# Chunk states of an SSD scan in three rounded products, split at the end of each chunk's front

## The chip, the core and the metric

The kernel runs on one core of one Trainium2 chip. Five engines work side by side, each through its own list of instructions: TensorE (PE, with its weight loads as PEld), VectorE (DVE), ScalarE (ACT), GpSimd (POOL) and SyncE (SP), which here only issues transfers. The metric is the device time of one execution in microseconds. Before the change it is 2855.78 us, the median of three runs between 2853.89 and 2859.62.

## The reference

The program is a two-layer decoder over 1024 tokens with 16 learned tokens in front (1040 in all), 1024 features, in float32. Layer 0 is a state-space mixer (SSD) with a gated convolutional feed-forward block, layer 1 a stick-breaking attention with another such block. The change touches only the scan inside the mixer:

```python
cb = jnp.einsum('bclgn,bcsgn->bgcls', c_c, b_c)
y_diag = jnp.einsum('bgcls,bgecls,bcsgep->bclgep', cb, decay_in, xdt)
decay_to_end = jnp.exp(a_cs[..., -1:] - a_cs)
chunk_states = jnp.einsum('bclgn,bgecl,bclgep->cbgepn', b_c, decay_to_end, xdt)
...
_, prev_states = lax.scan(step, ..., (chunk_states, chunk_decay))
y_off = jnp.einsum('bclgn,cbgepn,bgecl->bclgep', c_c, prev_states, jnp.exp(a_cs))
```

There are four groups of eight heads; a head has 64 channels and a state of 128 by 64. `chunk_states` is what a chunk of tokens adds to the state, `y_diag` what a chunk's tokens give each other, `y_off` what the state from earlier chunks gives them.

## The kernel before

The 1040 tokens are cut in two ways. Projections go over three token tiles of 348, 348 and 344; the scan goes over nine chunks, eight of 116 tokens and one of 112. `mixer` runs the scan of one group at a time, chunk by chunk, and fills each chunk with projection tiles of other groups: `SHARES` gives the number of tiles per chunk (mostly 2 in groups 0 and 3, a pattern of 4, 3, 3 in groups 1 and 2). One tile is 24 matmuls, three for each of eight blocks of features: `mm3` multiplies the rounded high part of the weights by the high and the low part of the data, and the low part of the weights by the high part of the data, all of type float32r. Its tiles are called `pj`; they take turns in three PSUM banks.

What comes out of a `pj` tile is convolved by one ACT instruction (L336) and three DVE instructions (L339) and passed through silu (L614), or, for the gate, goes through silu (L646) and is multiplied and squared (L653, L658, L662, L664). Weights of the next block are loaded ahead; ACT rounds them into `wh` (L196), POOL subtracts to get `wl`.

In this stretch the order on PE, DVE, ACT and POOL is the order in which the program is written: a manual schedule switches the framework's own ordering off. The order of one chunk c is:

- the front (`ssd_front`): PE makes `cb` and transposes b and x (`px`); ACT copies the transposed b into `bk` (L778); DVE makes `cbm`, `xdt` and the masked decays `D` (L780, L782, L783); POOL makes `xde`, which is `xdt` times the decay to the chunk's end, in two pieces of 256 columns (the helper's line, L102);
- the projection tiles of this chunk, with the decays of chunk c+1 between them: `D` is loaded, DVE subtracts and clips (L752, eight instructions), ACT takes the exponential (L753);
- the back (`ssd_back`): PE multiplies `S` = bk by xde (L799), then the products `y` (L810, L812); DVE adds `S` to the running state (L805; in chunk 0 ACT copies it, L803), then adds `y` into x (L814); POOL scales the state for the next chunk (`state`, two pieces).

POOL's product `E` for chunk c+1 (the factor of `y_off`, four pieces) stands, in groups 0 and 3, behind the scaled state of chunk c and in front of `xde` of chunk c+1. In most chunks of groups 1 and 2, which have three or four tiles, it has been made before.

Of the kernel before, what the change touches and what calls it, by code (L numbers as in the profile page):

```python
# [8 lines left out]
F32 = mybir.dt.float32  # L9
F32R = mybir.dt.float32r  # L10
AF = mybir.ActivationFunctionType
ALU = mybir.AluOpType

P = 128
# [7 lines left out]
CH = [(c * CB, min(CB, L - c * CB)) for c in range(9)]  # L22
# [32 lines left out]
GH = 8  # L55
# [36 lines left out]
def pieces(eng, out, x, y, op):  # L92

    n = out.shape[1]
    size = 1
    for d in out.shape[2:]:
        size *= d
    step = max(1, PIECE // size)
    done = []
    for a in range(0, n, step):  # L100
        c = slice(a, min(a + step, n))
        done.append(eng.tensor_tensor(out[:, c], x[:, c], y[:, c], op=op))  # L102
    return done


class Trunk:
# [652 lines left out]
    def ssd_front(self, g, x, bt, ct, c, dk, pool):  # L759

        nc = self.nc
        h0 = GH * g
        tt = nc.vector.tensor_tensor
        t0, n = CH[c]
        cc = 3 * (c % 3) + c // 3
        e = t0 + n
        pcb = self.sm("cb")
        if c < 8:
            nc.tensor.transpose(pcb[:n, P : 2 * P], bt[:, t0:e], self.ident)
        nc.tensor.matmul(pcb[:n, :n], bt[:, t0:e], ct[:, t0:e], start=True, stop=True)  # L770
        px = self.lg("px")
        for q in range(4):
            nc.tensor.transpose(px[:n, q * P : q * P + P], x[q][:, t0:e], self.ident)
        px = px[:n].rearrange("p (h d) -> p h d", h=GH)
        bk = xde = None
        if c < 8:
            bk = pool.tile([P, P], F32, tag="bk", name=self.nm("bk"), bufs=2)
            nc.scalar.activation(bk[:n], pcb[:n, P : 2 * P], AF.Copy)  # L778
        cbm = pool.tile([P, CB], F32, tag="cbm", name=self.nm("cbm"), bufs=2)
        tt(cbm[:n, :n], pcb[:n, :n], self.past[:n, :n], op=ALU.mult)  # L780
        xdt = pool.tile([P, GH, 64], F32, tag="xdt", name=self.nm("xdt"), bufs=2)
        tt(xdt[:n], px, self.cols[:n, 0, cc, h0 : h0 + GH].unsqueeze(2).to_broadcast([n, GH, 64]), op=ALU.mult)  # L782
        tt(dk, dk, cbm[:n, :n].unsqueeze(1).to_broadcast([n, GH, n]), op=ALU.mult)  # L783
        if c < 8:
            xde = pool.tile([P, GH, 64], F32, tag="xde", name=self.nm("xde"), bufs=2)
            pieces(nc.gpsimd, xde[:n], xdt[:n], self.cols[:n, 2, cc, h0 : h0 + GH].unsqueeze(2).to_broadcast([n, GH, 64]), ALU.mult)
        return xdt, xde, bk

    def ssd_back(self, g, x, c, dk, ce, xdt, xde, bk, states, pool):

        nc = self.nc
        h0 = GH * g
        t0, n = CH[c]
        cc = 3 * (c % 3) + c // 3
        e = t0 + n
        state, new = states
        if c < 8:
            ps = self.lg("S")
            nc.tensor.matmul(ps, bk[:n], xde[:n].rearrange("p h d -> p (h d)"), start=True, stop=True)  # L799
            psv = ps.rearrange("p (h d) -> p h d", h=GH)  # L800
            if c == 0:
                new = pool.tile([P, GH, 64], F32, tag="state", name=self.nm("state"), bufs=2)
                nc.scalar.activation(new, psv, AF.Copy)  # L803
            else:
                nc.vector.tensor_tensor(new, new, psv, op=ALU.add)  # L805
        py = self.sm("y")
        for i in range(GH):
            q, r = i // 2, 64 * (i % 2)
            y = py[r : r + 64, q * CB : q * CB + n]
            nc.tensor.matmul(y, xdt[:n, i, :], dk[:, i, :], start=True, stop=c == 0)  # L810
            if c:
                nc.tensor.matmul(y, state[:, i, :], ce[:, i, :], start=False, stop=True)  # L812
        for q in range(4):
            nc.vector.scalar_tensor_tensor(x[q][:, t0:e], x[q][:, t0:e], self.par("d_skip", 4 * g + q),  # L814
                                           py[:, q * CB : q * CB + n], op0=ALU.mult, op1=ALU.add)
        scaled = None
        if c < 7:
            scaled = pool.tile([P, GH, 64], F32, tag="state", name=self.nm("state"), bufs=2)
            cn = 3 * ((c + 1) % 3) + (c + 1) // 3
            pieces(nc.gpsimd, scaled, new, self.cd[:, cn, h0 : h0 + GH].unsqueeze(2).to_broadcast([P, GH, 64]), ALU.mult)  # L820
        return new, scaled
# [1236 lines left out]
```

## Time and profile before

| | |
|---|---|
| median of three runs | 2855.78 us |
| the profiled execution's own time | 2855.13 us |
| its span in the trace | 2853.3 us |
| PE busy | 2809.2 us, 98% of the span |
| DVE, ACT, POOL busy | 2065.4, 1580.2, 1578.6 us |
| share of PE in the chain that ended last | 91% |
| granted TensorE clock | 0.997 |
| scan of the four groups | from 114 to 613 us of the span |

The page gives busy time by engine and the chain of work that ended last; the timeline gives each engine's instructions in order with the idle time in front of each, and the name of what ended it. Columns of a timeline row are: start in us from the span's start, length in us, engine, line, operation, output and inputs, shapes, count, and in brackets the idle time before it. `S` is listed as two matmul records for each instruction (64 records for 32 chunks), because the hardware takes a float32 product in two records here.

### The profile page before, as it was taken

Reading aid. Unit: us, or ns where it says so; the run is one execution under the profiler, and the core shown is the slowest. Engines: PE = TensorE matmul, PEld = TensorE weight load, DVE = VectorE, ACT = ScalarE, POOL = GpSimd, SP = SyncE. Lnnn points to the kernel's source line nnn. Section 1 sums busy time; section 2 is a strip of 40 time slices with the busy share of each in tenths; the row PEclk is TensorE's granted clock in tenths of the full one; section 3 lists DMA queues with packets and bytes.
Section 4 is the critical chain, followed back from the end, with each engine's and each line's share of the span. In section 5 each row is a group of like instructions: output and inputs, shape, how many; then the busy total and the mean of one; then the engine's idle time right before and its main releaser. Section 6 shows DMA issues by size and latency. Waiting matters only on the chain.

```text
span 2853.3 us, 56464 instructions
## 1 busy us (share of the span) xinstructions
PE 2809.2 (98%) x21251; PEld 2691.9 (94%) x21251; DVE 2065.4 (72%) x3936; ACT 1580.2 (55%) x3077; POOL 1578.6 (55%) x2144
## 2 busy tenths in 40 slices
PE   8999999999999999999999999999999999999998
PEld 7989999999999999999999999999899999999888
DVE  5676666668487676767886888888749676766776
ACT  5554554543256555555335777777536555555433
POOL 2366455553519888867763212112254888886881
PEclk9999999999999999999999999999999999999999
DMA  4333333343413222235142222222532222225331
GB/s 119 86 112 93 121 83 125 116 136 101 120 64 96 78 80 78 79 135 176 49 142 77 74 73 69 80 70 57 184 131 77 82 80 82 75 82 185 111 104 67
DMA packets 141740, 281.78 MB, mean 99 GB/s; under 512 B 16307, under 2 KB 71740, under 8 KB 141468
## 3 DMA queue, kind: packets, MB, share of 16 engines
q1 hardware_dynamic: 135844, 267.01, 29.8%
q0 software_dynamic: 2048, 6.49, 0.6%
q10 hardware_dynamic: 3576, 4.67, 0.5%
q8 instruction: 168, 2.75, 0.4%
q14 instruction: 104, 0.85, 0.1%
HBM read 207.79 MB, written 55.42 MB: 92 GB/s over the span
## 4 chain that ended last, share of the span: by engine, by line
PE 91%; DVE 4%; ACT 2%; POOL 1%; issue 1%; DMA 0%; SPq 0%; ACTq 0%; DVEq 0%; POOLq 0%
PE p L209 10%; PE p L210 10%; PE p L211 10%; PE acc L209 8%; PE acc L211 8%; PE acc L210 8%; PE pj L209 8%; PE pj L210 8%; PE pj L211 8%; PE po L1710 3%; PE lg L1653 2%; PE wT L1687 2%; PE y L810 1%; PE S L799 1%; PE y L812 1%; PE ms L1069 1%
## 5 line engine op out<-in xcount | busy, mean ns | idle before, releaser
L102 POOL TENSOR_TENSOR wl<-w,wh 128x256 fp32r<-128x256 f32 x760 | 678.9, 923 | 352.2 <-ACT wh L196 225.4
L209 PE MATMUL pj<-uh,wh 128*128 128x348 f32 (+2 forms) x1536 | 500.4, 326 | 2.1 <-DVE xbc L339 1.4
L210 PE MATMUL pj<-ul,wh 128*128 128x348 f32 (+2 forms) x1536 | 494.9, 322 | 0.8 <-DVE ul L320 0.8
L211 PE MATMUL pj<-uh,wl 128*128 128x348 f32 (+2 forms) x1536 | 492.0, 320 | 0.0
L209 PE MATMUL p<-bh,fh 128*128 128x262 f32 (+1 forms) x1408 | 400.9, 285 | 3.9 <-DVE p L1237 3.7
L211 PE MATMUL p<-bh,fl 128*128 128x262 f32 (+1 forms) x1408 | 401.0, 285 | 0.9 <-POOL fl L102 0.9
L210 PE MATMUL p<-bl,fh 128*128 128x262 f32 (+1 forms) x1408 | 399.2, 284 | 0.0
L102 POOL TENSOR_TENSOR fl<-x,fh 128x256 fp32r<-128x256 f32 x352 | 264.3, 783 | 186.8 <-ACT fh L1174 160.9
L210 PE MATMUL p<-bl,wh 128*128 128x262 f32 (+1 forms) x1040 | 295.6, 284 | 1.1 <-DVE bl L1098 1.1
L209 PE MATMUL p<-bh,wh 128*128 128x262 f32 (+1 forms) x1040 | 295.3, 284 | 0.4 <-ACT ft L1234 0.4
L211 PE MATMUL p<-bh,wl 128*128 128x262 f32 (+1 forms) x1040 | 294.1, 283 | 0.0
L209 PEld LDWEIGHTS pj<-uh,wh 128*128 128x128 f32 x1536 | 288.7, 188 | 4.5 <-ACT xbc L336 1.7
L210 PEld LDWEIGHTS pj<-ul,wh 128*128 128x128 f32 x1536 | 289.2, 188 | 2.4 <-DVE ul L320 1.4
L211 PEld LDWEIGHTS pj<-uh,wl 128*128 128x128 f32 x1536 | 288.7, 188 | 0.1
L339 DVE SCALAR_TENSOR_TENSOR c<-p,params,c 128x260 f32<-128x260 f32 (+1 forms) x528 | 248.4, 480 | 54.7 <-ACT c L336 48.3
L209 PEld LDWEIGHTS p<-bh,fh 128*128 128x128 f32 x1408 | 268.0, 191 | 4.7 <-DVE p L1237 4.1
L211 PEld LDWEIGHTS p<-bh,fl 128*128 128x128 f32 x1408 | 267.1, 190 | 1.6 <-POOL fl L102 1.5
L210 PEld LDWEIGHTS p<-bl,fh 128*128 128x128 f32 x1408 | 267.8, 190 | 0.5 <-DVE bl L1098 0.4
L1234 ACT ACTIVATE ft<-p 128x262 f32<-128x262 f32 (+1 forms) x352 | 133.2, 382 | 179.9 <-DVE p L1237 110.1
L210 PE MATMUL acc<-gl,wh 128*128 128x260 f32 (+1 forms) x672 | 214.2, 320 | 0.0
L211 PE MATMUL acc<-gh,wl 128*128 128x260 f32 (+1 forms) x672 | 213.2, 319 | 0.0
L209 PE MATMUL acc<-gh,wh 128*128 128x260 f32 (+1 forms) x672 | 210.8, 320 | 0.1
(336 smaller groups left out, 7690.6 us busy)
## 6 DMA issues: line engine op xcount, KB each, us to landing
w<-in_w_up SPq DMA_DIRECT2D x88, 512.0 KB
w<-in_w_down SPq DMA_DIRECT2D x44, 512.0 KB
w<-in_w_in SPq DMA_DIRECT2D x40, 512.0 KB
E<-ea_d SPq DMA_DIRECT2D x32, 464.0 KB
D<-acs_d SPq DMA_DIRECT2D x32, 420.5 KB
g<-c SPq DMA_DIRECT2D x88, 130.0 KB
g<-c SPq DMA_DIRECT2D x88, 128.0 KB
b<-g SPq DMA_DIRECT2D x16, 520.0 KB
```

Of the source, the lines that this page charges most:

```text
L102: done.append(eng.tensor_tensor(out[:, c], x[:, c], y[:, c], op=op))
L209: self.behind(mm(out, wh, uh, start=first, stop=False, skip_group_check=joins), tie, "behind the sums of squares")
L210: mm(out, wh, ul, start=False, stop=False, skip_group_check=joins)
L211: self.last_mm = mm(out, wl, uh, start=False, stop=last, skip_group_check=joins)
L339: ins = nc.vector.scalar_tensor_tensor(out, ps[:, o + i : o + i + n], wcol(i), out, op0=ALU.mult, op1=ALU.add)
L799: nc.tensor.matmul(ps, bk[:n], xde[:n].rearrange("p h d -> p (h d)"), start=True, stop=True)
L810: nc.tensor.matmul(y, xdt[:n, i, :], dk[:, i, :], start=True, stop=c == 0)
L812: nc.tensor.matmul(y, state[:, i, :], ce[:, i, :], start=False, stop=True)
L1234: nc.scalar.activation(s[:, :N], ps[:, :N], AF.Copy)
L1653: nc.tensor.matmul(ps[:nt, a, :m], part[:, c0 : c0 + nt], ks[a][:, s0 : s0 + m], start=x == 0, stop=x == 1)
L1687: nc.tensor.transpose(pt[:ns, x * CB : x * CB + nt], bt[:nt, a, x * CB : x * CB + ns], self.ident[:nt, :nt])
L1710: nc.tensor.matmul(po[64 * a : 64 * a + 64, t0:n], v[: CH[c][1], c, 64 * a : 64 * a + 64], wt[a][q][: CH[c][1], r, t0:n], start=x == 0, st ...
```

## The change

`bk` becomes two float32r tiles: ACT's rounded copy, and DVE's difference of the PSUM original and that copy. `xde` becomes three tiles: POOL's float32 product as before, ACT's rounded copy `xdh` of it, and DVE's difference `xdl`. The two are written right behind POOL's product, at the end of the front. `S` is made by `mm3` from these parts, and stands behind the products `y` instead of in front of them. The new tiles have one buffer each where `bk` and `xde` had two.

```diff
-            bk = pool.tile([P, P], F32, tag="bk", name=self.nm("bk"), bufs=2)
-            nc.scalar.activation(bk[:n], pcb[:n, P : 2 * P], AF.Copy)
+            bk = pool.tile([P, 2, P], F32R, tag="bk", name=self.nm("bk"), bufs=1)
+            nc.scalar.activation(bk[:n, 0], pcb[:n, P : 2 * P], AF.Copy)
+            tt(bk[:n, 1], pcb[:n, P : 2 * P], bk[:n, 0].bitcast(F32), op=ALU.subtract)
...
-            xde = pool.tile([P, GH, 64], F32, tag="xde", name=self.nm("xde"), bufs=2)
-            pieces(nc.gpsimd, xde[:n], xdt[:n], self.cols[...], ALU.mult)
+            xde = [pool.tile([P, GH, 64], dt, tag=t, name=self.nm(t), bufs=1) for t, dt in (("xdh", F32R), ("xdl", F32R), ("xde", F32))]
+            pieces(nc.gpsimd, xde[2][:n], xdt[:n], self.cols[...], ALU.mult)
+            self.split_xde(xde, c)
         return xdt, xde, bk
+
+    def split_xde(self, xde, c):
+
+        hi, lo, t = (t[: CH[c][1]] for t in xde)
+        self.nc.scalar.activation(hi, t, AF.Copy)
+        self.nc.vector.tensor_tensor(lo, t, hi.bitcast(F32), op=ALU.subtract)
...
-        if c < 8:
-            ps = self.lg("S")
-            nc.tensor.matmul(ps, bk[:n], xde[:n].rearrange("p h d -> p (h d)"), start=True, stop=True)
-            ... (copy or add into the state)
         py = self.sm("y")
         for i in range(GH):
             ... (the products y)
+        if c < 8:
+            ps = self.lg("S")
+            hi, lo = (t[:n].rearrange("p h d -> p (h d)") for t in xde[:2])
+            self.mm3(ps, bk[:n, 0], bk[:n, 1], hi, lo, True, True)
+            ... (copy or add into the state, unchanged)
```

Three places show what this does to the order. The first is PE at the end of chunk 0 of group 0; `pj` rows end the projection tiles, `cb` and `px` begin chunk 1. Before:

```order
L211 MATMUL pj_1263<-uh_156,wl_1061 128x348
L799 MATMUL S_1302<-xde_1226,bk_1219 128x512
L810 MATMUL y_1306<-D_1161,xdt_1223 64x116 x8
L769 MATMUL cb_1326<-ident,xbc_967 116x128
L770 MATMUL cb_1326<-xbc_1067,xbc_967 116x116
```

Now:

```order
L211 MATMUL pj_1268<-uh_156,wl_1061 128x348
L809 MATMUL y_1307<-D_1161,xdt_1224 64x116 x8
L209 MATMUL S_1316<-xdh_1227,bk_1219 128x512
L210 MATMUL S_1316<-xdl_1228,bk_1219 128x512
L211 MATMUL S_1316<-xdh_1227,bk_1219 128x512
L769 MATMUL cb_1333<-ident,xbc_967 116x128
L770 MATMUL cb_1333<-xbc_1067,xbc_967 116x116
```

One instruction became three, and they moved from before the eight y rows to behind them.

The second is ACT in group 0, from the exponential of chunk 2's decays to that of chunk 3's; L336 takes a projection tile out of PSUM. Before:

```order
L753 ACTIVATE D_1384<-D_1384 116x928
L778 ACTIVATE bk_1466<-cb_1458 116x128
L336 ACTIVATE xbc_1353<-pj_1476,params 128x344
L614 ACT_TABLE_LOAD
L614 ACTIVATE xbc_1353<-xbc_1353 128x348
L196 ACTIVATE wh_1512<-w_170_1510 128x1024
L336 ACTIVATE xbc_1519<-pj_1520,params 128x348
L614 ACTIVATE xbc_1353<-xbc_1353 128x344
L753 ACT_TABLE_LOAD
L753 ACTIVATE D_1506<-D_1506 116x928
```

Now:

```order
L753 ACTIVATE D_1396<-D_1396 116x928
L778 ACTIVATE bk_1480<-cb_1472 116x128
L794 ACTIVATE xdh_1488<-xde_1490 116x512
L336 ACTIVATE xbc_1365<-pj_1495,params 128x344
L614 ACT_TABLE_LOAD
L614 ACTIVATE xbc_1365<-xbc_1365 128x348
L196 ACTIVATE wh_1531<-w_176_1529 128x1024
L336 ACTIVATE xbc_1538<-pj_1539,params 128x348
L614 ACTIVATE xbc_1365<-xbc_1365 128x344
L753 ACT_TABLE_LOAD
L753 ACTIVATE D_1525<-D_1525 116x928
```

One row is new: the copy `xdh` stands between `bk` and the first tile that ACT takes out of PSUM.

The third is DVE in the same chunk, from one addition to the state to the next. Before:

```order
L805 TENSOR_TENSOR state_1319<-state_1319,S_1427 128x512
L814 SCALAR_TENSOR_TENSOR xbc_867<-xbc_867,params,y_1430 128x116
L780 TENSOR_TENSOR cbm_1468<-cb_1458,past 116x116
L782 TENSOR_TENSOR xdt_1470<-px_1461,cols 116x512
L783 TENSOR_TENSOR D_1384<-D_1384,cbm_1468 116x928
L339 SCALAR_TENSOR_TENSOR xbc_1353<-pj_1476,params,xbc_1353 128x344 x3
L339 SCALAR_TENSOR_TENSOR xbc_1519<-pj_1520,params,xbc_1519 128x348 x3
L752 TENSOR_SCALAR D_1506<-D_1506,cols 116x116 x8
L805 TENSOR_TENSOR state_1451<-state_1451,S_1559 128x512
```

Now (of the four rows L823, which were L814, the last is shown, as above):

```order
L821 TENSOR_TENSOR state_1326<-state_1326,S_1456 128x512
L823 SCALAR_TENSOR_TENSOR xbc_867<-xbc_867,params,y_1439 128x116
L779 TENSOR_TENSOR bk_1480<-cb_1472,bk_1480 116x128
L781 TENSOR_TENSOR cbm_1483<-cb_1472,past 116x116
L783 TENSOR_TENSOR xdt_1485<-px_1475,cols 116x512
L784 TENSOR_TENSOR D_1396<-D_1396,cbm_1483 116x928
L795 TENSOR_TENSOR xdl_1489<-xde_1490,xdh_1488 116x512
L339 SCALAR_TENSOR_TENSOR xbc_1365<-pj_1495,params,xbc_1365 128x344 x3
L339 SCALAR_TENSOR_TENSOR xbc_1538<-pj_1539,params,xbc_1538 128x348 x3
L752 TENSOR_SCALAR D_1525<-D_1525,cols 116x116 x8
L821 TENSOR_TENSOR state_1465<-state_1465,S_1595 128x512
```

Two rows are new: the low part of `bk` in front of `cbm`, and `xdl` between the decays and the convolution of the chunk's first tile. POOL's list is the same as before, row by row.

More of the change, by code (lines that the diff above doesn't have):

```diff
@@ L784, in ssd_front @@
         if c < 8:
-            xde = pool.tile([P, GH, 64], F32, tag="xde", name=self.nm("xde"), bufs=2)
-            pieces(nc.gpsimd, xde[:n], xdt[:n], self.cols[:n, 2, cc, h0 : h0 + GH].unsqueeze(2).to_broadcast([n, GH, 64]), ALU.mult)
+            xde = [pool.tile([P, GH, 64], dt, tag=t, name=self.nm(t), bufs=1) for t, dt in (("xdh", F32R), ("xdl", F32R), ("xde", F32))]
+            pieces(nc.gpsimd, xde[2][:n], xdt[:n], self.cols[:n, 2, cc, h0 : h0 + GH].unsqueeze(2).to_broadcast([n, GH, 64]), ALU.mult)
+            self.split_xde(xde, c)
         return xdt, xde, bk
+    def split_xde(self, xde, c):
+        hi, lo, t = (t[: CH[c][1]] for t in xde)
+        self.nc.scalar.activation(hi, t, AF.Copy)
+        self.nc.vector.tensor_tensor(lo, t, hi.bitcast(F32), op=ALU.subtract)
     def ssd_back(self, g, x, c, dk, ce, xdt, xde, bk, states, pool):
@@ L796, in ssd_back @@
         state, new = states
-        if c < 8:
-            ps = self.lg("S")
[L799 to L805, printed above, removed]
         py = self.sm("y")
@@ L812, in ssd_back @@
                 nc.tensor.matmul(y, state[:, i, :], ce[:, i, :], start=False, stop=True)
+        if c < 8:
+            ps = self.lg("S")
+            hi, lo = (t[:n].rearrange("p h d -> p (h d)") for t in xde[:2])
+            self.mm3(ps, bk[:n, 0], bk[:n, 1], hi, lo, True, True)
+            psv = ps.rearrange("p (h d) -> p h d", h=GH)
+            if c == 0:
+                new = pool.tile([P, GH, 64], F32, tag="state", name=self.nm("state"), bufs=2)
+                nc.scalar.activation(new, psv, AF.Copy)
+            else:
+                nc.vector.tensor_tensor(new, new, psv, op=ALU.add)
         for q in range(4):
```

## The prediction

> **What bounds the kernel now.** I read the page's busy time first, then busy time by stretch, then the timeline of each engine through one chunk of the scan. The page says that PE is nearly always at work:
>
> ```profile
> PE 2809.2 (98%) x21251; PEld 2691.9 (94%) x21251; DVE 2065.4 (72%) x3936; ACT 1580.2 (55%) x3077; POOL 1578.6 (55%) x2144
> ```
>
> The change lies wholly in the scan, so the stretches of its four groups matter; the first number after the window is its length, then come PE, PEld, DVE, ACT and POOL:
>
> ```profile
> 120.00:213.00 93.00, 90.50 (x722) 82.35 (x721) 72.64 (x181) 55.45 (x75) 58.87 (x82) 1.00 0.35 102
> 213.00:360.00 147.00, 147.00 (x1086) 138.60 (x1082) 94.76 (x224) 74.32 (x111) 79.29 (x106) 1.00 0.36 104
> 506.00:613.00 107.00, 106.61 (x821) 98.04 (x821) 68.78 (x168) 57.82 (x88) 73.22 (x96) 1.00 0.39 122
> ```
>
> PE sets the time there too, so a shorter product on PE is worth its full length as long as the other engines keep up. DVE is idle 20.4 us in group 0 (93.00 - 72.64), some 2.5 us in each of eight chunks; in group 1 it is idle 52.2 us, 5.8 us in each of nine. What each engine does in one chunk of group 0 shows who is near the edge. DVE, from one addition to the state to the next:
>
> ```profile
> 150.27 0.68 DVE L805 TENSOR_TENSOR state<-state,S 128x512 f32<-128x512 f32 x1
> ...
> 152.03 0.69 DVE L782 TENSOR_TENSOR xdt<-px,cols 116x512 f32<-116x512 f32 x1
> 152.63 1.27 DVE L783 TENSOR_TENSOR D<-D,cbm 116x928 f32<-116x928 f32 x1
> 154.45 1.81 DVE L339 SCALAR_TENSOR_TENSOR xbc<-pj,params,xbc 128x348 f32<-128x348 f32 x3 [0.55 <-ACT xbc L336]
> 158.29 1.80 DVE L339 SCALAR_TENSOR_TENSOR xbc<-pj,params,xbc 128x344 f32<-128x344 f32 x3 [2.02 <-ACT xbc L336]
> 160.00 1.60 DVE L752 TENSOR_SCALAR D<-D,cols 116x116 f32<-116x116 f32 x8
> 161.51 0.68 DVE L805 TENSOR_TENSOR state<-state,S 128x512 f32<-128x512 f32 x1
> ```
>
> The period is 161.51 - 150.27 = 11.24 us, of which DVE idles 0.55 + 2.02 = 2.57 us, both times for a tile that PE had just finished. POOL in the same chunk:
>
> ```profile
> 151.10 1.19 POOL L102 TENSOR_TENSOR state<-state,cd 128x256 f32<-128x256 f32 x2 [2.32 <-DVE state L805]
> 152.24 3.50 POOL L102 TENSOR_TENSOR E<-E,xbc 128x232 f32<-128x232 f32 x4
> 155.71 1.18 POOL L102 TENSOR_TENSOR xde<-xdt,cols 116x256 f32<-116x256 f32 x2
> 162.34 1.19 POOL L102 TENSOR_TENSOR state<-state,cd 128x256 f32<-128x256 f32 x2 [5.46 <-DVE state L805]
> ```
>
> After each addition to the state, POOL scales it, makes E and only then xde, which ends at 156.89, 6.62 us behind the start of the addition. POOL then waits 5.46 us: before the change nothing but PE's S needs xde, and S comes at the chunk's end. ACT:
>
> ```profile
> 151.27 0.26 ACT L778 ACTIVATE bk<-cb 116x128 f32<-116x128 f32 x1
> 153.78 0.64 ACT L336 ACTIVATE xbc<-pj,params 128x348 f32<-128x348 f32 x1 [2.24 <-PE pj L211]
> 154.44 1.28 ACT L614 ACT_TABLE_LOAD   x1
> 155.73 0.50 ACT L614 ACTIVATE xbc<-xbc 128x348 f32<-128x348 f32 x1
> 157.62 0.64 ACT L336 ACTIVATE xbc<-pj,params 128x344 f32<-128x344 f32 x1 [1.39 <-PE pj L211]
> ...
> 162.68 1.05 ACT L196 ACTIVATE wh<-w 128x1024 fp32r<-128x1024 f32 x1
> ```
>
> It takes the chunk's first tile out of PSUM at 153.78, three microseconds before xde exists.
>
> **The change part by part.** On PE, one float32 product becomes three of float32r:
>
> ```profile
> 202.14 0.33 PE L210 MATMUL pj<-ul,wh 128*128 128x352 f32 x1
> 202.31 0.32 PE L211 MATMUL pj<-uh,wl 128*128 128x352 f32 x1
> 202.47 1.02 PE L799 MATMUL S<-xde,bk 116*128 116x512 f32 x2
> 203.42 0.43 PE L810 MATMUL y<-D,xdt 116*64 116x116 f32 x4
> ```
>
> S holds PE 0.95 us until y begins. A float32r product of 352 columns starts 0.16 us after the one before it, so 512 columns take about 0.235 us and three 0.70 us: 0.25 us less. Some of the 0.95 us is the step to y's smaller tiles, which stays; I take 0.2 us saved per chunk. The bounds are a gain of 0.3 us, and a loss of 0.5 us if a 512-column float32r product takes as long as one of S's two records (0.475 us). Over 32 chunks 0.2 us would be 6 us, where PE sets the time. [...]
>
> New work on ACT and DVE is priced from operations like it:
>
> ```profile
> L803 ACT ACTIVATE state<-S x4: 580/592/596, 128.3 to 521.7; 128x512 f32<-128x512 f32 x4
> ...
> L926 DVE TENSOR_TENSOR y<-t,yh x36: 499/518/1056, 622.3 to 705.2; 128x348 fp32r<-128x348 f32 x24, 128x344 fp32r<-128x344 f32 x12
> ...
> L780 DVE TENSOR_TENSOR cbm<-cb,past x36: 264/272/279, 120.5 to 605.3; 116x116 f32<-116x116 f32 x32, 112x112 f32<-112x112 f32 x4
> ```
>
> The copy xdh has the width of L803: 0.59 us (bounds 0.26, the narrow bk copy, and 1.05, the wide wh). The difference xdl is L926 at 512 columns instead of 348, near the 0.69 us of xdt: I take 0.65 (bounds 0.52 and 0.69). The low part of bk is like cbm, 0.2 us of extra issue. Busy time alone, 0.85 us on DVE, would fit into its 2.57 us.
>
> What does not fit is the place. xdh waits for xde, and everything written behind it on ACT waits too: both tiles that ACT takes out of PSUM, the weights' rounding, the next exponential. xdl stands in front of all six L339 and the eight L752, which stand in front of the next addition to the state, which releases POOL's next state, E and xde. This closes a ring that had been open. [...]
>
> Once around the ring in group 0, counted from the start of an addition to the state: state, E and xde as before, to 6.62; xdh to 7.25, call it h; xdl from 7.3 to 7.95, where DVE had been free since 3.63 (154.45 less the wait of 0.55 is 153.90). ACT takes the first tile at h, loads its table, does its silu, and takes the second at h + 2.35 (0.66 + 1.29 + 0.4 by the spacing of the rows); L339 of the second tile starts 0.67 later at h + 3.0, L752 1.71 later, the addition 1.51 later: h + 6.25. That is 13.5 us. In two chunks of three an L196 of 1 us stands before the first or the second L336, which makes 14.5. The mean is 14.2 us against 11.24, 2.9 us a chunk, and PE, waiting for E and xdl, must follow: it has three banks, one chunk's tiles ahead at most.
>
> Group 0 also loses at its start, where there is no E yet:
>
> ```profile
> 121.50 2.00 POOL L102 TENSOR_TENSOR xde<-xdt,cols 116x256 f32<-116x256 f32 x2 [14.46 <-DVE xdt L782]
> ...
> 128.32 0.58 ACT L803 ACTIVATE state<-S 128x512 f32<-128x512 f32 x1
> ...
> 138.65 0.68 DVE L805 TENSOR_TENSOR state<-state,S 128x512 f32<-128x512 f32 x1
> ...
> 195.30 0.68 DVE L805 TENSOR_TENSOR state<-state,S 128x512 f32<-128x512 f32 x1
> ```
>
> xde ends at 123.7 instead of 123.5, xdl at 125.05, so the six L339 begin 2.7 us late and the second three wait for ACT; the state copy moves from 128.32 to 131.65. Then state, E, xde and xdh of chunk 1 end at 138.7 and its addition starts at 145.95 instead of 138.65. Five rings of 14.2 put that of chunk 6 at 217 instead of 195.30. S of chunk 7 then starts at 217 + 7.3 = 224.3 instead of 202.47: **+22 us** for group 0.
>
> In group 3 E again stands between state and xde:
>
> ```profile
> 543.82 0.67 DVE L805 TENSOR_TENSOR state<-state,S 128x512 f32<-128x512 f32 x1
> ...
> 551.98 0.51 DVE L653 TENSOR_TENSOR xbc<-xbc,z 128x344 f32<-128x344 f32 x1
> 552.41 1.60 DVE L752 TENSOR_SCALAR D<-D,cols 116x116 f32<-116x116 f32 x8
> 553.93 0.68 DVE L805 TENSOR_TENSOR state<-state,S 128x512 f32<-128x512 f32 x1
> ...
> 545.78 4.06 POOL L102 TENSOR_TENSOR E<-E,xbc 128x232 f32<-128x232 f32 x4
> ```
>
> Here two gate tiles follow: a table load of 1.28, then two rounds of silu, square and two DVE products of about 0.5 us each, handed to and fro (some 1.5 us a round), then L752: about h + 6, a ring of 13.3 us, a little more with L196. PE's own period for two tiles is the 11.24 us of group 0. Chunk 6 has less on DVE and runs shorter. Six rings, less what chunks 6 and 7 make up, give **+8 us**.
>
> In groups 1 and 2 E is out of the way:
>
> ```profile
> 300.79 2.00 POOL L102 TENSOR_TENSOR xde<-xdt,cols 116x256 f32<-116x256 f32 x2 [0.52 <-DVE xdt L782]
> ```
>
> xde starts as soon as xdt is there, DVE waits some 1.7 us plus 0.65, and its 5.8 us of idle time cover that. PE keeps its pace and saves 0.2 us in 16 chunks: **-3 us**. If that cover were gone, each of these chunks would lose up to 1 us.
>
> The sum is 22 + 8 - 3 = 27 us on the profiled execution's 2855.13 us (span 2853.3 and 1.8 around it): 2882 us. The median of the runs is 0.65 us above that execution, so I predict 2883 us. With xdh and xdl at their bounds a ring moves by -0.5 to +0.5 us, over 13 rings 6 us each way; PE's price adds up to 8 us on the slow side. The likeliest case's own range is 2874 to 2896.
>
> **The rivals.** First, the waits are covered: DVE and ACT have idle time, PE has three banks, and PE's saving counts in full, 0.2 us in each of 32 chunks: 2849 us. The 72% of DVE speak for it; the ring of 13.5 us and more against PE's 11.24 speaks against it. It decides at the ring: below 11 us this rival holds.
>
> Second, the ring is there but shorter. E took 3.50 us while DVE's own work ran beside it; at the 0.59 us a piece of state and xde it would be 2.4 us, and DVE now stands still for part of it. A ring of 13.1 us loses 1.9 us a chunk: 16 in group 0, 4 in group 3, less 3: 2873 us, and 2865 if L196 also finds room. Against it: the slow part of E lies under L783, which stays.
>
> Third, groups 1 and 2 close a ring as well, through the next exponential, L196, wl and E: 15.1 us or so against a period near 15. At 1 us in twelve chunks this adds 12 us and takes the 3 us away: 2898 us. Their idle time speaks against it.
>
> **How the numbers follow.** I give the forecast 0.55, the shorter ring 0.2, the third rival 0.13 and the first 0.12. The range of 2857 to 2903 us leaves out the first rival and a little at either end. About 0.2%, 5.7 us, is what a measurement here can tell from no change: faster has the first rival's chance, 0.12; within 0.2% needs a ring hardly above PE's period, 0.06; slower is the rest, 0.82.
>
> **What would show it.** In the changed profile xdh should start when xde ends, some 6.6 us behind the addition to the state, with ACT idle before it for POOL; DVE should idle about 3.5 us before xdl in groups 0 and 3; additions to the state should stand 13 to 14.5 us apart in group 0; PE should idle in front of y or S there, by 2 us or more a chunk, and hardly in groups 1 and 2; three S rows should take 0.7 us. I am wrong if additions in group 0 stay 11.2 us apart, or if PE does not wait there, or if groups 1 and 2 grow by as much as group 0.

## The result

The changed kernel takes 2907.51 us (median of four runs, 2904.71 to 2908.72) against 2855.55 us (2853.89 to 2859.62) for the kernel before on the same chip: a ratio of 1.0177, 95% interval 1.0163 to 1.0191. It is slower, by 52 us where 27 were forecast, and lies 4.5 us above the upper end of the range.

The page of the changed kernel: busy time, then the chain of waits.

```profile
PE 2828.9 (97%) x21283; PEld 2714.1 (93%) x21283; DVE 2103.3 (72%) x4000; ACT 1597.0 (55%) x3109; POOL 1576.3 (54%) x2144
...
PE 79%; DVE 9%; ACT 6%; POOL 4%; issue 2%; DMA 0%; ACTq 0%; DVEq 0%; SPq 0%; POOLq 0%
```

The shares of busy time hardly moved: 97% of a longer span for PE, still 72% for DVE. What changed is how engines wait for each other; the chain is no longer PE's almost alone. Busy time by stretch, cut at the start of each group's first `px` and at the end of the last `y` (length, then PE, PEld, DVE, ACT, POOL, the granted clock, and the DMA share and rate):

```profile
113.80:237.80 124.00, 106.20 (x768) 95.43 (x767) 83.00 (x214) 62.30 (x86) 59.32 (x82) 0.95 0.29 81
237.80:389.40 151.60, 148.50 (x1086) 142.44 (x1085) 103.85 (x238) 77.26 (x118) 77.94 (x106) 0.98 0.35 100
389.40:539.90 150.50, 147.62 (x1087) 141.57 (x1086) 104.97 (x234) 76.44 (x118) 77.96 (x106) 0.99 0.38 108
539.90:662.10 122.20, 112.63 (x843) 104.61 (x842) 75.29 (x185) 62.14 (x95) 69.74 (x94) 0.96 0.36 105
```

PE now idles 18 us in group 0 and 10 us in group 3, and 3 us in each of groups 1 and 2, where it had none. The next table has the length of each group in each kernel's trace (start of `px` in chunk 0 to the same in the next group; for group 3 to the start of the last `y`); the kernels of the experiments are told below.

| kernel | group 0 | group 1 | group 2 | group 3 | after the last y | time, us |
|---|---|---|---|---|---|---|
| before | 98.8 | 146.3 | 146.4 | 107.5 | 2239.5 | 2855.55 |
| the change | 124.0 | 151.6 | 150.5 | 122.2 | 2243.2 | 2907.51 |
| split later, everywhere | 105.5 | 145.5 | 145.5 | 111.2 | 2239.8 | 2862.43 |
| split later, groups 1 and 2 | 123.6 | 145.4 | 145.5 | 123.4 | 2240.3 | 2892.12 |
| split later, chunk 6 of groups 1 and 2 | 124.0 | 147.7 | 150.6 | 123.5 | 2237.3 | 2900.25 |
| E behind xde | 110.5 | 150.3 | 151.7 | 113.6 | 2237.4 | 2878.55 |
| split not read | 123.7 | 152.3 | 150.7 | 122.4 | 2237.3 | 2903.99 |
| no wl in groups 1 and 2 | 123.8 | 145.4 | 145.5 | 122.0 | 2238.6 | 2891.76 |
| no wl in group 3 | 123.7 | 150.4 | 151.8 | 115.0 | 2239.0 | 2894.68 |
| PE's gaps filled | 123.9 | 150.1 | 150.2 | 127.1 | 2244.5 | 2910.85 |
| only S behind y | 97.7 | 146.7 | 146.7 | 107.1 | 2245.2 | 2857.23 |
| split later and E behind xde | 99.7 | 145.4 | 145.5 | 109.8 | 2238.8 | 2855.58 |
| mixed | 98.0 | 145.1 | 145.1 | 107.1 | 2244.4 | 2853.45 |

From before to the change the groups grow by 25.2, 5.3, 4.1 and 14.7 us, 49.3 in all. The first group begins 1.0 us earlier, and the unchanged program behind the last `y` took 3.7 us more: 52.0, the difference of the spans (2905.3 - 2853.3). The column behind the last `y` moves between 2237 and 2245 us from kernel to kernel, so one trace's total can't be trusted to 4 us. The groups can be trusted to some 1.3 us each: groups 1 and 2 take 150.3 and 151.7, 150.4 and 151.8 us in the two kernels that change only groups 0 and 3 or only group 3, against 151.6 and 150.5 in the change.

**Group 0** is the forecast ring. One chunk, POOL, ACT and DVE of the changed kernel's timeline:

```profile
173.77 1.19 POOL L102 TENSOR_TENSOR state<-state,cd 128x256 f32<-128x256 f32 x2 [7.62 <-DVE state L821]
174.92 3.54 POOL L102 TENSOR_TENSOR E<-E,xbc 128x232 f32<-128x232 f32 x4
178.42 1.18 POOL L102 TENSOR_TENSOR xde<-xdt,cols 116x256 f32<-116x256 f32 x2
...
179.63 0.63 ACT L794 ACTIVATE xdh<-xde 116x512 fp32r<-116x512 f32 x1 [5.42 <-POOL xde L102]
180.17 1.04 ACT L196 ACTIVATE wh<-w 128x1024 fp32r<-128x1024 f32 x1
181.11 0.63 ACT L336 ACTIVATE xbc<-pj,params 128x348 f32<-128x348 f32 x1
...
172.95 0.68 DVE L821 TENSOR_TENSOR state<-state,S 128x512 f32<-128x512 f32 x1
...
180.29 0.69 DVE L795 TENSOR_TENSOR xdl<-xde,xdh 116x512 fp32r<-116x512 f32 x1 [3.66 <-ACT xdh L794]
...
187.35 0.69 DVE L821 TENSOR_TENSOR state<-state,S 128x512 f32<-128x512 f32 x1
```

xdh starts 6.68 us behind the addition to the state, ACT having idled 5.42 us for POOL; xdl finds DVE idle for 3.66 us; ACT takes the first tile out of PSUM (L336) at 181.11, 1.5 us behind xdh's start, where before the change it did so three microseconds ahead of xde. This ring, with an L196 in it, takes 14.40 us.

**Groups 1 and 2**, where no ring was forecast, have one too. From one addition to the state to the next in group 1 (DVE, ACT, POOL of the changed kernel's timeline):

```profile
327.25 0.68 DVE L821 TENSOR_TENSOR state<-state,S 128x512 f32<-128x512 f32 x1
...
332.67 0.69 DVE L795 TENSOR_TENSOR xdl<-xde,xdh 116x512 fp32r<-116x512 f32 x1 [1.75 <-ACT xdh L794]
333.28 3.59 DVE L339 SCALAR_TENSOR_TENSOR xbc<-pj,params,xbc 128x344 f32<-128x344 f32 x6
336.79 3.81 DVE L752 TENSOR_SCALAR D<-D,cols 116x116 f32<-116x116 f32 x8
342.18 1.81 DVE L339 SCALAR_TENSOR_TENSOR xbc<-pj,params,xbc 128x348 f32<-128x348 f32 x3 [1.58 <-ACT xbc L336]
343.91 0.68 DVE L821 TENSOR_TENSOR state<-state,S 128x512 f32<-128x512 f32 x1
...
333.45 1.05 ACT L196 ACTIVATE wh<-w 128x1024 fp32r<-128x1024 f32 x1
...
340.64 0.98 ACT L753 ACTIVATE D<-D 116x928 f32<-116x928 f32 x1 [3.74 <-DVE D L752]
...
334.57 2.81 POOL L102 TENSOR_TENSOR wl<-w,wh 128x256 fp32r<-128x256 f32 x4 [2.60 <-ACT wh L196]
337.34 2.62 POOL L102 TENSOR_TENSOR E<-E,xbc 128x232 f32<-128x232 f32 x4
```

DVE is the ring by itself here: it waits 1.75 us for xdh, makes xdl, runs six L339, then eight L752 in 3.81 us, waits for the exponential and the third tile's L336, and only then adds to the state: 16.66 us, where PE needs 14.99. In the kernel before, the same ring took 14.81 us (298.27 to 313.08). Its DVE rows from the second tile on, and POOL's:

```profile
305.63 1.81 DVE L339 SCALAR_TENSOR_TENSOR xbc<-pj,params,xbc 128x348 f32<-128x348 f32 x3 [2.05 <-ACT xbc L336]
307.36 2.42 DVE L752 TENSOR_SCALAR D<-D,cols 116x116 f32<-116x116 f32 x8
311.35 1.81 DVE L339 SCALAR_TENSOR_TENSOR xbc<-pj,params,xbc 128x348 f32<-128x348 f32 x3 [1.57 <-ACT xbc L336]
...
303.16 2.83 POOL L102 TENSOR_TENSOR wl<-w,wh 128x256 fp32r<-128x256 f32 x4 [0.36 <-ACT wh L196]
305.95 2.61 POOL L102 TENSOR_TENSOR E<-E,xbc 128x232 f32<-128x232 f32 x4
```

The wait for xdh (1.75 us), xdl (0.61 to the next start) and the low part of bk (0.20) take the place of DVE's wait of 2.05 us for the second tile, which is gone: 0.5 us more. The other 1.4 us are L752, 3.81 in place of 2.42: before, wl was done when L752 began and only E's second half ran beside it; now the end of wl and all of E do. The wait of 1.57 us ahead of the third tile is as long as before.

DVE falls 1.7 us further behind in such a chunk until PE's three banks are full. PE's wait for a bank comes in the next chunk, chunk 6 with its four tiles, which takes 23.0 us in place of 18.9. Its row in PE's timeline:

```profile
351.88 0.40 PE L209 MATMUL pj<-uh,wh 128*128 128x348 f32 x1 [2.44 <-DVE xbc L339]
```

Behind this wait the granted clock is 0.50 from 352.6 to 355.8 us, an estimated 1.6 us of PE's work; wait and clock together make about the 4.1 us.

**Group 3** has rings of 15.1, 13.4, 15.0, 15.1, 11.4 and 15.8 us (additions to the state from 567.80 to 653.57).

### The profile page after: what moved, and what is told of

It is laid out like the page before. It is cut to its first block, busy times and chain, and to the rows that moved or that the text cites. A ratio compares the mean times of both kernels' runs of the same rounds, so it can differ in the third digit from the quotient of the medians.

```text
span 2905.3 us, 56657 instructions
## 1 busy us (share of the span) xinstructions
PE 2828.9 (97%) x21283; PEld 2714.1 (93%) x21283; DVE 2103.3 (72%) x4000; ACT 1597.0 (55%) x3109; POOL 1576.3 (54%) x2144
## 4 chain that ended last, share of the span: by engine, by line
PE 79%; DVE 9%; ACT 6%; POOL 4%; issue 2%; DMA 0%; ACTq 0%; DVEq 0%; SPq 0%; POOLq 0%
PE p L211 10%; PE p L210 10%; PE p L209 10%; PE acc L209 8%; PE acc L211 8%; PE acc L210 8%; PE pj L209 5%; PE pj L210 5%; PE pj L211 5%; PE po L1719 3%; PE lg L1662 2%; PE wT L1696 2%; DVE D L752 2%; POOL E L102 1%; DVE xbc L339 1%
## 5 line engine op out<-in xcount | busy, mean ns | idle before, releaser
L339 DVE SCALAR_TENSOR_TENSOR c<-p,params,c 128x260 f32<-128x260 f32 (+1 forms) x528 | 248.7, 480 | 53.2 <-ACT c L336 46.4
L1243 ACT ACTIVATE ft<-p 128x262 f32<-128x262 f32 (+1 forms) x352 | 133.6, 383 | 186.9 <-DVE p L1246 109.8
```

The costliest lines, as they stand in the source:

```text
L339: ins = nc.vector.scalar_tensor_tensor(out, ps[:, o + i : o + i + n], wcol(i), out, op0=ALU.mult, op1=ALU.add)
L1243: nc.scalar.activation(s[:, :N], ps[:, :N], AF.Copy)
```

## The experiments

**The split later.** The two instructions of the split go from the end of the front to the place behind the chunk's first projection tile.

```diff
-            self.split_xde(xde, c)
...
                                 dk, ce = next(ahead)
+                                if c < 8:
+                                    self.split_xde(ops[1], c)
```

> The two instructions xdh (ACT) and xdl (DVE) are written behind the chunk's first projection tile instead of in front of it, in all 32 chunks; all else is as changed. If the place of the split closes the ring, and so makes the loss, ACT takes its first tile out of PSUM before xde exists, xdh finds ACT idle at about 6.7 us behind the addition to the state, xdl falls into DVE's idle 2 us ahead of its second three L339, additions to the state in group 0 stand 11.0 to 11.3 us apart again, and the saving on PE is left: 32 times 0.2 us below the kernel before, 2849 us. If instead the loss comes from the three products on PE, or from the added 0.63 + 0.69 us on ACT and DVE as such, it stays above 2890 us.

Measured: 2862.43 us, ratio 1.0025 (1.0016 to 1.0034). 45 of the 52 us are gone, with the same products on PE and the same work on ACT and DVE, so the place of the split makes most of the loss. But 2849 us was missed: groups 1 and 2 save 0.9 us each and not 1.6, and groups 0 and 3 are still 6.7 and 3.7 us longer than before. Of the first five rings, those without an L196 take 11.2 us, the others 11.7 to 12.5. ACT in one of the longer rings:

```profile
182.14 0.63 ACT L793 ACTIVATE xdh<-xde 116x512 fp32r<-116x512 f32 x1 [1.99 <-POOL xde L102]
182.68 1.04 ACT L196 ACTIVATE wh<-w 128x1024 fp32r<-128x1024 f32 x1
183.63 0.63 ACT L336 ACTIVATE xbc<-pj,params 128x348 f32<-128x348 f32 x1
```

L196 still waits behind xdh, and the second tile behind L196.

**The split later in some groups or chunks only.** The same edit under a condition; in the second of these kernels it is `g in (1, 2) and c == 6`.

```diff
+            if not (g in (1, 2)):
+                self.split_xde(xde, c)
...
+                                if c < 8 and (g in (1, 2)):
+                                    self.split_xde(ops[1], c)
```

> The split is written behind the first projection tile in groups 1 and 2 only; groups 0 and 3 keep it at the end of the front. In the trace of the change groups 1 and 2 take 5.3 and 4.1 us more than before, 4.1 us of each in chunk 6 with its four tiles. If that too comes from the split's place, both groups end some 3 us below the kernel before, and the time is 2907.5 - 9.4 - 3.2 = 2895 us. If it comes from something that runs through the whole scan (the granted clock, which fell to 0.98 there), it stays at 2903 us or above.

Measured: 2892.12 us, ratio 1.0128 (1.0114 to 1.0141). Groups 1 and 2 fall to 145.4 and 145.5 us, below the kernel before; groups 0 and 3 stay long. The loss of groups 1 and 2 was the split's place too, as none of it is left. L752 still takes 3.81 us in the ring that answers to the one above, and the additions still stand 15.75 us apart (322.13 to 337.88); but DVE falls only 0.8 us behind PE there, and PE doesn't wait in these two groups.

> The split is written behind the first projection tile in one chunk only of groups 1 and 2, chunk 6, which has four tiles of the input projection; the other 30 chunks keep it at the end of the front. If the 4.1 us that each of these two chunks lost come from PE's wait for a bank (2.4 us for the products L339 that stand behind xdl, and a step before it), both come back and the time is 2907.5 - 8.2 = 2899 us. If the loss of groups 1 and 2 is spread over their chunks and only shows there, it comes up again in a later chunk and the time stays above 2904 us.

Measured: 2900.25 us, ratio 1.0155 (1.0141 to 1.0169). The time agrees with the first theory, the trace does not. Group 1 gets 4.0 us back, but group 2 nothing: its chunk 6 falls from 23.1 to 18.8 us while its chunk 3, also of four tiles, grows from 20.0 to 24.4. Much of the fall in time is the part behind the scan (2237.3 us in place of 2243.2). So the loss isn't chunk 6's own: DVE's lag stays and comes up in another chunk of four tiles.

**E behind xde.** The split stays in the front; POOL's order is changed. `next(ahead)` is L752 and the exponential, where they are still to come, and the loop behind the front makes E.

```diff
-                        for _ in ahead:
-                            pass
+                        if steps < 2:
+                            next(ahead)
                         ops = self.ssd_front(g, x, bt, ct, c, dk, pool)
+                        for _ in ahead:
+                            pass
```

> The split stays at the end of the front, but POOL makes E behind xde instead of in front of it (groups 0 and 3, where E is made between two chunks). If the closed ring is the cause, it gets shorter by about E's 3.5 us less the wait for xdt: xde ends 4.5 us behind the addition to the state, xdh at 5.1, the next addition at 11.4, or 12.3 where the rounding of weights stands in between, mean 11.7 against 14.2; group 0 gets back some 17 us and group 3 some 8, and with the 9 us of groups 1 and 2 left the time is 2880 to 2885 us. If the cause is the split's work or the products on PE, nothing changes: 2905 us or more.

Measured: 2878.55 us, ratio 1.0079 (1.0066 to 1.0092), 29 us back. Group 0 gets 13.5 us and group 3 8.6 us back. xdh starts 4.76 us behind the addition to the state (166.90 to 171.66) and this ring, with an L196, takes 12.5 us (to 179.39), 12.3 expected. Rings in which L196 stands at its other place take 12.9 us, so the first five average 12.3 and not the 11.7 expected, and group 0 gets back less than the 17 us expected. The ring runs over POOL's E.

**The split made, but not read.** S is one float32 product again, behind y.

```diff
+            nc.scalar.activation(bk[:n, 2].bitcast(F32), pcb[:n, P : 2 * P], AF.Copy)
...
-            self.mm3(ps, bk[:n, 0], bk[:n, 1], hi, lo, True, True)
+            nc.tensor.matmul(ps, bk[:n, 2].bitcast(F32), xde[2][:n].rearrange("p h d -> p (h d)"), start=True, stop=True)
```

> Everything that ACT, DVE and POOL do in the changed kernel stays, at its place, but PE does not read it: S is one float32 product from xde behind y, from an own float32 copy of bk that ACT makes (0.26 us more in each chunk). xdh, xdl and both parts of bk are made and read by nobody. If the loss comes from what stands in order behind xdh on ACT and behind xdl on DVE, it stays: 2907.5 us plus up to 32 times 0.16 us for the product where PE sets the pace, and up to 0.26 us a ring for the copy, 2906 to 2918 us. If PE's wait for xdh and xdl in front of S makes the loss (12.4 us of PE's waits are for these two), the time falls to 2895 us or below.

Measured: 2903.99 us, ratio 1.0177 (1.0162 to 1.0193); the groups are as long as in the change to 0.7 us. (The median lies 2 us below the 2906 expected; in the profiled execution the part behind the scan took 5.9 us less.) PE's waits in this kernel's scan (engine, line, what it waited for, us in total, times, longest):

```profile
PE y L810 <- DVE D L785: 22.0, 10, 6.0
...
PE S L815 <- POOL xde L102: 3.7, 7, 0.5
```

Nobody reads xdh and xdl, and nearly the whole loss stays. It comes from the order on ACT and DVE. (That the new tiles have one buffer each is no cause of its own: the kernel with the split later and E behind xde, below, has them too and loses nothing.) In the changed kernel PE's waits name xdh and xdl for 12.4 us, but they only show where PE happened to stand:

```profile
PE y L809 <- DVE D L784: 11.4, 6, 5.0
PE S L209 <- ACT xdh L794: 9.9, 10, 1.2
PE pj L209 <- DVE xbc L339: 4.9, 2, 2.4
...
PE S L210 <- DVE xdl L795: 2.5, 11, 0.2
```

**Without wl, in groups 1 and 2 and in group 3.** POOL doesn't subtract, and the third product reads `wh`; `short` holds in groups 1 and 2 in the one kernel, in group 3 in the other.

```diff
+        if self.short:
+            wh = self.wp.tile([P, 1024], F32R, tag="wh", name=self.nm("wh"))
+            self.behind(nc.scalar.activation(wh[:, :n], w32[:, :n], AF.Copy), self.copy_tie, "behind the tiles in front")
+            return wh, wh
```

> The changed kernel, and for the weights that are read during groups 1 and 2 POOL's subtraction wl is left out (wh stands in for wl in the third product of these tiles, so the result is another); the rounding L196 on ACT stays. In the trace of the change a ring is closed in groups 1 and 2 too: additions to the state of chunks 4 and 5 of group 1 stand 16.66 us apart, where PE needs 14.99, and DVE's eight L752 take 3.5 to 3.8 us there beside POOL's wl and E, where they take 1.6 alone. If that is what closes the ring, it falls below 15 us without wl, PE sets the pace again, groups 1 and 2 take 145.5 us each instead of 151.6 and 150.5, and the time is about 2896 us. If the ring is closed by xdh's place alone, L752 beside wl or not, they stay above 149 us and the time above 2904 us.

Measured: 2891.76 us, ratio 1.013 (1.0116 to 1.0144); of the 4 us below the 2896 expected, the part behind the scan may be the cause, which took 4.6 us less than in the change. Groups 1 and 2 take 145.4 and 145.5 us: PE sets the pace again though the split is where the change put it. DVE and POOL in the ring that answers to the one above:

```profile
328.14 3.51 DVE L345 SCALAR_TENSOR_TENSOR xbc<-pj,params,xbc 128x344 f32<-128x344 f32 x6
331.57 1.60 DVE L758 TENSOR_SCALAR D<-D,cols 116x116 f32<-116x116 f32 x8
...
326.98 3.08 POOL L102 TENSOR_TENSOR E<-E,xbc 128x232 f32<-128x232 f32 x4 [0.33 <-DMA E<-ea_d]
```

The eight subtractions (L752, here L758) take 1.60 in place of 3.81 us. Without wl in front of it, E too has moved to where DVE works on L339, so the run takes both away from L752 and can't tell their shares. The wait for xdh is still there (1.74 us), but the additions stand 14.5 us apart (321.93 to 336.47).

> The changed kernel, and for the weights that are read during group 3 POOL's subtraction wl is left out (wh stands in for wl, so the third product of these tiles is another than the reference's); the rounding L196 on ACT stays. In the trace of the change the rings of group 3 with L196 in them take 15.0 to 15.1 us, that without it 13.4; 1.04 of the 1.6 us is L196 itself, and DVE's L664 takes 1.07 instead of 0.52 us beside POOL's wl. If the two engines slow each other down there, these rings fall to 14.5 us and the time by 2 to 4 us, to 2904 to 2906 us. If L196's place on ACT is all, they stay at 15 us and the time at 2907 us.

Measured: 2894.68 us, ratio 1.0132 (1.0116 to 1.0147), 13 us less where 2 to 4 were expected. Group 3 gets 7.2 us back, and the part behind it 4.2, which may be chance. The rings are 13.6, 13.4, 14.4, 13.5, 11.4 and 13.8 us. The end of the first ring, in the change and without wl:

```profile
579.41 1.06 DVE L653 TENSOR_TENSOR xbc<-xbc,z 128x348 f32<-128x348 f32 x1
580.39 2.58 DVE L752 TENSOR_SCALAR D<-D,cols 116x116 f32<-116x116 f32 x8
...
578.29 3.47 POOL L102 TENSOR_TENSOR wl<-w,wh 128x256 fp32r<-128x256 f32 x4 [3.84 <-ACT wh L196]
```

```profile
576.79 0.52 DVE L659 TENSOR_TENSOR xbc<-xbc,z 128x348 f32<-128x348 f32 x1
577.22 1.60 DVE L758 TENSOR_SCALAR D<-D,cols 116x116 f32<-116x116 f32 x8
```

I had counted one L664 at 0.5 us. That holds for one of the three rings with L196; in the other two it is L653 and the eight L752 that pay, 0.5 and 1.0 us in this ring. Of the three, wl made 1.5, 0.6 and 1.5 us, and L196 itself, which I had put at 1.04 us in each, only 0.1 to 1.0: the three take 13.6, 14.4 and 13.5 us without wl.

**PE's gaps filled.** The lines stand ahead of y, and the same with `ps` ahead of S.

```diff
+        fill = 4 if g in (0, 3) and 0 < c < 8 else 0
+        for _ in range(fill):
+            nc.tensor.matmul(py[:, :P], self.ident, self.ident, start=True, stop=True)
```

> The changed kernel, and in groups 0 and 3 PE is given eight small matmuls more in each of chunks 1 to 7 (four 128 x 128 float32 products ahead of y, four ahead of S, written into banks that y and S overwrite; nothing else reads them), some 2 us of work in the gaps in which it waits. If the lower granted clock (0.95 and 0.96 there) is a cost of its own, the clock comes back to 1.00 and the time falls by 5 to 12 us although PE has more to do, to 2896 to 2902 us. If only the ring over POOL, ACT and DVE sets these groups, the clock may come back, but additions to the state stay 14.2 us apart in group 0 and the time stays at 2907 us to within 3; if PE was the bound in some chunks, it rises by up to 2 us in each of them.

Measured: 2910.85 us, ratio 1.019 (1.0177 to 1.0203). The granted clock comes back from 0.95 to 0.98 in group 0 and from 0.96 to 0.99 in group 3 (windows of this kernel's trace):

```profile
113.00:238.00 125.00, 116.58 (x889) 106.88 (x888) 82.72 (x211) 63.04 (x87) 59.21 (x82) 0.98 0.29 82
...
540.00:664.00 124.00, 119.40 (x913) 112.77 (x912) 75.37 (x184) 61.27 (x93) 70.32 (x95) 0.99 0.34 104
```

Group 0 stays at 123.9 us. Groups 1 and 2, where nothing was filled and the clock rose to 1.00, get 1.5 and 0.3 us shorter: chunk 6 takes 21.5 us in both, in place of 23.0 and 23.1, but chunk 3 grows by 0.6 and 1.3 us, so most of what the clock gives PE waits for DVE again. Group 3 grows by 4.9 us, presumably because PE does more. So the full clock brings 1.9 us back in the first three groups, and the lower one is no main cause there. What it costs in group 3 this run can't tell.

**Only S behind y.** The kernel before, with the block of S moved.

```diff
-        if c < 8:
-            ps = self.lg("S")
...
         py = self.sm("y")
...
+        if c < 8:
+            ps = self.lg("S")
```

> Only the place of the product on PE is changed: the kernel before with its one float32 product S behind the products y, no split, no product of rounded parts. If the order on PE carries no cost, it is the kernel before to within 4 us, 2852 to 2859 us, and PE's period in chunks of groups 1 and 2 is what it was before (14.84 and 15.12 us). If waiting with S takes part in the loss (the addition to the state is released later), it is above 2862 us.

Measured: 2857.23 us, ratio 1.0006 (0.9997 to 1.0015), no difference. Group 0 gains 1.1 us; a chunk of three tiles in group 1 takes 14.89 us (229.16 to 244.05) in place of 14.83: the new order costs PE about 0.05 us.

**Split later and E behind xde.** Both edits above together.

> Both at once: the split behind the chunk's first projection tile, and E made behind xde. With the split late alone, the additions to the state in group 0 still stand 12.5 us apart where the rounding of weights (L196, 1.0 us) comes between xdh and ACT's second tile, 11.2 where it does not. With E behind xde, xde ends 2.2 us earlier, xdh is done before ACT is asked for the rounding, and PE alone sets the pace: 0.13 us less in each chunk than before, as groups 1 and 2 showed with the split late, 4 us in 32 chunks: 2851 us. If E comes too late for y there instead, PE waits for it up to 1 us in each of 13 chunks: 2860 us or more.

Measured: 2855.58 us, ratio 1.0002 (0.9993 to 1.0011): the loss is gone, and there is no gain. Groups 1 and 2 save 0.9 us each; group 0 takes 1.0 and group 3 2.3 more; PE's waits in this trace are 2.4 us once for `D` and 1.6 for E, and what else these two groups pay was not followed up. In it and in the kernel with S moved alone, PE's rows of S in one chunk of group 1 (first this kernel, then that one):

```profile
278.96 0.50 PE L209 MATMUL S<-xdh,bk 116*128 116x512 f32 x1
279.30 0.39 PE L210 MATMUL S<-xdl,bk 116*128 116x512 f32 x1
279.53 0.39 PE L211 MATMUL S<-xdh,bk 116*128 116x512 f32 x1
279.76 0.27 PE L769 MATMUL cb<-ident,xbc 128*116 128x128 f32 x1
```

```profile
277.07 1.12 PE L806 MATMUL S<-xde,bk 116*128 116x512 f32 x2
278.03 0.27 PE L769 MATMUL cb<-ident,xbc 128*116 128x128 f32 x1
```

From S to cb three products take 0.80 us, one float32 product 0.96: 0.16 us saved, less the 0.05 of the new order.

**Mixed.** Groups 0 and 3 with one float32 product behind y, groups 1 and 2 with three in front of y and the later split; `chunk_state` holds the block of S, with the one kind or the other.

```diff
+        if g in (1, 2):
+            new = self.chunk_state(g, c, n, bk, xde, new, pool)
         py = self.sm("y")
...
+        if g not in (1, 2):
+            new = self.chunk_state(g, c, n, bk, xde, new, pool)
...
+                                if c < 8 and g in (1, 2):
+                                    self.split_xde(ops[1], c)
```

> A version from the parts that gained: in groups 0 and 3 one float32 product S behind y and no split; in groups 1 and 2 three products in front of y, and the split behind the chunk's first projection tile. From the traces: S behind y alone took 1.1 us off group 0 and 0.4 off group 3; three products save 0.16 us where PE sets the pace, 16 times 0.16 = 2.6 us in groups 1 and 2. Together 4.1 us below the kernel before, 2851 us, 0.14%, hardly more than can be told. If xdl then comes too late for S in front of y, or the added 1.3 us a chunk on ACT and DVE cost something there, it is at the kernel before or above it.

Measured: 2853.45 us, ratio 0.9994 (0.9985 to 1.0003). In the trace the four groups are 3.7 us shorter than before, near the 4.1 expected, but it can't be told from no change: a version that beats the kernel before was not found.

## Why the prediction was right, and where it failed

- **The sign and, for groups 0 and 3, the mechanism** were right: the split's place closes a ring over POOL, ACT and DVE, and what stands behind xdh and xdl pays. The signs named for it are in group 0's rows, except that some of its rings take 14.8 us (14.5 named) and that three S rows take 0.80 us where PE doesn't wait (0.7 named). That the order on the engines is the cause, and not PE's reading of xdh and xdl, the split that nobody reads shows; that the ring runs over POOL's E, the run with E behind xde. The ring rests on ACT and DVE keeping to the written order even where later work is ready, and the rows show it for both. ACT idled 5.42 us until xdh started at 179.63, with the chunk's first L336 written behind it, whose last product on PE had ended at 174.03. Before the change DVE idled 2.02 us until 158.29 with eight L752 written behind; their `D` had been asked for at 138.39, and nothing moved by DMA from 147.0 to 149.0, so it had landed.
- **Group 0, +22 us**: the ring was sized right. Five rings from 144.71 to 215.59 average 14.18 us, 14.2 forecast; S of chunk 7 starts at 222.94, 224.3 forecast, in a group that began 1.0 us earlier. The sum stopped there. Chunk 7's own ring still stands in front of chunk 8's xdt, and PE then waits 5.0 us for `D` (1.5 before), so the group ends 25.2 us late.
- **Groups 1 and 2, -3 us, "DVE waits some 1.7 us plus 0.65, and its 5.8 us of idle time cover that": the step that failed**, by 12.4 of the 22 us missed in the groups (the other 3 us of the miss lie outside them). The wait was sized right (1.75 and 0.69 us), the rest was not. First, the 5.8 us are an average over chunks; the ring shown above had 3.62 us of idle time before the change. The 2.05 us of it ahead of the second tile did cover, the 1.57 us ahead of the third did not: they wait for the exponential, which waits for DVE's own L752, and so move along with the delay. Second, and more: L196 starts 6.2 us behind the addition in place of 3.8, which moves wl and E beside L752, and L752 takes 1.4 us more; the prediction left it as it was. Without that the ring would be an estimated 15.3 us (16.66 - 1.39), hardly above PE's 14.99; at 16.66 us it exceeds it by 1.7. So both are needed: with the split later, or without wl, PE doesn't wait. This is the third rival in kind. Its path through the exponential was right; its 15.1 us left L752 as it was, and its 1 us a chunk didn't follow from 15.1 us against 15.
- **Group 3, +8 us**: 14.7, a term sized too small. Without wl it is 7.5 us. The 13.3 us of a ring without L196 were right (13.4); "a little more with L196" was 1.6 to 1.7 us in three of the first four rings, and in two of these nearly all of that, in the third a good third, is not L196 but DVE's slower work beside POOL's wl, which follows it. Chunks 6 and 7, which were to make up for some of it, took 27.2 us together in place of 23.9.
- **PE's saving, 0.2 us a chunk**: 0.16 us for the products and 0.11 with the new order, seen in groups 1 and 2 wherever PE set the pace. Had the first rival held, it would have given 3.5 us and not 6.
- **The second rival**, a shorter ring because DVE stands still beside E, did not occur: E took 3.54 us in place of 3.50.

## What to carry to other kernels

Before a new instruction is written into an engine that keeps to the written order, as ACT did here (5.42 us idle ahead of xdh with a finished tile's L336 behind it), ask what it waits for and follow everything written behind it once around: here 1.3 us of work a chunk, on engines that were busy 55 and 72% of the time, cost 52 us, and the same work behind the next tile 7. An engine's idle time covers a delay only if what ends that idle time does not itself wait for the delayed work. And price the operations of a moved ring with their new neighbours: the largest miss came mostly from a DVE operation that got slower when another engine's work had moved beside it (eight L752, 3.81 us in place of 2.42).

## What the hardware showed beyond that

- Eight L752 of DVE took 3.81 us beside the end of POOL's wl and all of its E, 2.42 us beside half of E (the kernel before, at 307.36) and 1.60 us alone (the kernel before, at 160.00), although they share no data with POOL there. The eight of the changed kernel one by one (count: shortest, median and longest in ns):

```profile
L752 DVE TENSOR_SCALAR D<-D,cols x8: 270/690/725, 336.8 to 340.3; 116x116 f32<-116x116 f32 x8
```

  The five that started beside wl and E took 0.67 to 0.73 us each, the three behind E's end 0.27. Single pieces of wl and E last 0.73 to 0.74 and 0.68 to 0.70 us, about as long as each of the five. Why an L752 takes so long there the rows can't show.
- In chunk 8 of group 0 PE idled 4.98 us (the changed kernel's timeline of PE; the first row is from a chunk without such a gap):

```profile
178.77 0.42 PE L809 MATMUL y<-D,xdt 116*64 116x116 f32 x4
...
233.86 0.75 PE L809 MATMUL y<-D,xdt 112*64 112x112 f32 x4 [4.98 <-DVE D L784]
...
234.66 0.69 PE L809 MATMUL y<-D,xdt 112*64 112x112 f32 x4
```

  Behind the gap four records of y take 0.69 us where they take 0.42 else, and the granted clock is 0.50 from 233.1 to 239.8 us. Shorter gaps came before such a clock too: it was 0.50 from 195.5 to 198.8 us, where no gap in the 20 us ahead was longer than 1.2 us, and behind the 2.44 us in chunk 6 of group 1. With the gaps filled in groups 0 and 3, two waits like that last one stayed (4.8 us together, the longer one 2.4) and the mean clock of groups 1 and 2 was 1.00, so the single gap doesn't decide. Filling brought most of the clock back (0.95 to 0.98 in group 0, 0.96 to 0.99 in group 3) and not the time.
- Of the three float32r products of 512 columns shown above, the first one behind the y products (weights of 64 columns) took 0.34 us to the next one's start, the others 0.23.
